# One-engine norm chains, heads with k outermost, and later table steps in a nine-layer block on one core

## The chip, the cores and the metric

The kernel runs on one core of a Trainium2 chip. The metric is the device time of one execution in microseconds. A core has the engines PE (matrix multiplication), DVE (VectorE), ACT (ScalarE) and POOL (GpSimd), and SP, which here only issues DMA transfers.

## The reference

Two blocks of two layers work on x, 512 tokens of 1024 channels, in float32. Every layer is a mixer or a feed-forward part with a residual sum and a normalisation over the channels; cut to what matters:

```
rms_norm(x, g) = x * rsqrt(mean(x*x, -1) + eps) * g
# first block: pool mixer, ffn, attention, ffn, each of them:
m = mixer_or_ffn(rms_norm(x, pre_g))
x = x + rms_norm(m, post_g)
# ffn: u = h @ w_in; width-3 causal conv + bias; gelu(gate) * val; @ w_out
# second block, modulated by a condition c: s5 mixer, mlp, ssd mixer, mlp
h = rms_norm(x, g) * (1 + scale) + shift
x = x + gate * y(h)
# last: rms_norm(x, final_g)
```

The s5 mixer needs powers and phasors of a complex matrix, which depend on the weights alone ("tables").

## The kernel before, in words

The channels lie on the partitions: x is eight tiles (k = 0 to 7) of 128 channels by 512 tokens. Each product is made of three matmuls of rounded halves, `hi*hi`, `lo*hi`, `hi*lo` (L219, L220, L221); the weights' halves `wh`, `wl` are made by ACT (L204) and DVE (L205). The layers are pool, ffn0, attn, ffn1, s5, mlp0, ssd, mlp1 and a final norm.

Between two layers stands a seam (`seam`), in halves of 256 tokens: the tail of the layer before for a half, then for the first block `chain` (`post_add`): a sum of squares of the tail's output `f` (`Norm.add`), its root by two tiny matmuls against ones and a diagonal (`Norm.rs`: L306, ACT's root L309, DVE's reciprocal L310 and diagonal `dg` L313, L319, and ACT's copy to `rs`, L321), then per k tile a scaling of `f` (L449, L450) and the sum into x (L453), and the squares of the new x. For an ffn or attention behind it (`PreScale`) `h` is x times a gain, split into `hi` (ACT, L427) and `lo` (DVE, L428), and the root is applied to the outputs (`un` or `u` times `rsx`, L979 and L952). For the second block (`PreNorm`) `h` needs the root first: L397, L400, `hi` L401, `lo` L402. Alternate k tiles go to POOL and DVE (`engs`); the sums of squares have one accumulator on each (L296). Then the head: the first four (ssd: five) output tiles of the next layer, by halves (`Held.run`), 192 matmuls of 128x256. Two output tiles q = 0, 1 share a PSUM bank; the code takes all k of q = 0, then of q = 1, bank after bank.

The code's order isn't the order on the engines. A scheduler that simulates the engines puts every instruction in a fixed place in its engine's queue; the chains have a raised priority. An engine works through its queue in order, so an instruction that waits holds what is behind it.

The tables of s5 are generators whose steps (up to a `yield`) are taken by the layers: in the pool layer once (`work(1)`), in ffn0 `rate` steps behind each group and one behind each tile of a down projection. A group is two gate and two value tiles: 96 matmuls of 128x512 into four banks, and four `u` (L952). ffn0 has eleven groups (the first is the head's) in three phases, with a down projection after each.

Of the kernel before, what the change touches and what calls it, by code (L numbers as in the profile page):

```python
# [63 lines left out]
def net_kernel(ctx: ExitStack, tc: tile.TileContext, I: dict, out: bass.AP, parts=ALL):  # L64
# [165 lines left out]

    def project(W, k0, nk, c0, tiles, xh, xl, evac, **kw):

        for n in range(tiles[0], tiles[1], 2):
# [44 lines left out]
    class Norm:  # L278
        def __init__(self):
            self.acc = {}  # L280
            self.seen = set()

        def add(self, tile_, span, eng):
            a, b = span
            if eng not in self.acc:
                self.acc[eng] = tt("acc")
            dst = self.acc[eng][:, a:b]
            if (eng, a) not in self.seen:
                self.seen.add((eng, a))
                if span == FULL:  # L290
                    self.seen.add((eng, HALVES[1][0]))
# [6 lines left out]
        def rs(self, span, eps, out=None):  # L298
# [15 lines left out]
            if nb == 2:  # L314
                p2 = ps[:, 256:]
            else:
                p2 = psn.tile([P, 512], F32, tag="n", name=nm("pn"))
# [53 lines left out]
    class PreNorm:  # L371
# [15 lines left out]
        def run(self, span):  # L387
# [25 lines left out]
    class PreScale(PreNorm):  # L413
# [16 lines left out]
        def run(self, span):  # L430
            if self.rs is None:
                self.rs = xp.tile([P, S], F32, tag="rsx", name=nm("rsx"))
            self.norm.rs(span, self.eps, out=self.rs)

    def engs(k):
        return G if k % 2 else V

    def post_add(ft, sq, gname, g0, span, nxt, pre):

        ts = slice(*span)  # L440
        for k in POOL_K:
            A.activation(ft[k][:, ts], ft[k][:, ts], AF.Copy, scale=vc(gname, g0 + k))
# [113 lines left out]
    def s5_powers(pool, dr, pr, pi, cr, ci, sg, far, near):  # L556
# [1496 lines left out]
```

## Time and profile before

| | us |
|---|---|
| median of three runs | 2519.96 (2519.84 to 2521.32) |
| the profiled execution | 2522.2 |
| its span, first to last instruction | 2520.5 |
| PE busy | 2358.8 (94%) |
| DVE busy | 1717.7 (68%) |
| ACT busy | 1151.8 (46%) |
| POOL busy | 454.9 (18%) |

The time outside the span is 1.7 us. The mean granted clock of TensorE is 0.968 of full. PE's busy time contains matmuls at the lower of its two clocks and matmuls whose ends are modelled, so it is read together with the granted clock and the start times of neighbours. An engine's idle time is named with what released it: `<-DVE u L952 14.2` means 14.2 us of waiting that ended with DVE's operation of line 952.

### The profile page before, as it was taken

To read this page: it belongs to the slowest core of one execution; us is meant where nothing else is said; L and a number is where in the kernel's file an instruction comes from. 1 tells how busy PE (TensorE), PEld (TensorE's weight loads), DVE (VectorE), ACT (ScalarE), POOL (GpSimd) and SP (SyncE) were. 2 spreads that over 40 slices of the span, in tenths; PEclk is the share of its full clock that TensorE was granted. 3 is DMA by queue.
4 is the path that set the end of the run, shared out by engine and by line. 5 is a ranking of instruction groups with operands and counts; after the bars stand their busy time and mean duration, and the time that the engine had idled before them with its cause. 6 is when DMAs were issued, how large, how long until landed. Compare 5 with 4: busy or idle time off the path is not lost.

```text
span 2520.5 us, 33869 instructions
## 1 busy us (share of the span) xinstructions
PE 2358.8 (94%) x12485; PEld 1986.4 (79%) x12485; DVE 1717.7 (68%) x2969; ACT 1151.8 (46%) x2070; POOL 454.9 (18%) x489
## 2 busy tenths in 40 slices
PE   6889999988889999996899999999999999999998
PEld 5767777876677888886878887788877888888888
DVE  6895987677858778777654666666778788633333
ACT  6443534467676444354543432333555554422322
POOL 2202131131321000014111210112133432301110
PEclk9989999989999999997999999999999999999999
DMA  4234443312094555551952356543333332233322
GB/s 123 67 100 131 125 138 112 122 43 67 27 231 136 176 175 167 184 176 56 304 158 76 114 167 195 178 149 97 110 101 97 111 103 82 91 100 97 96 88 72
DMA packets 297782, 311.32 MB, mean 124 GB/s; under 512 B 53569, under 2 KB 251025, under 8 KB 296593
## 3 DMA queue, kind: packets, MB, share of 16 engines
q1 hardware_dynamic: 270033, 278.22, 35.5%
q10 hardware_dynamic: 23680, 17.31, 2.3%
q0 software_dynamic: 3904, 13.63, 1.6%
q8 instruction: 98, 1.61, 0.3%
q14 instruction: 67, 0.55, 0.1%
HBM read 284.92 MB, written 24.18 MB: 123 GB/s over the span
## 4 chain that ended last, share of the span: by engine, by line
PE 70%; DVE 12%; DMA 7%; ACT 5%; issue 4%; POOL 1%; SPq 0%; DVEq 0%; ACTq 0%; POOLq 0%
PE mm L220 20%; PE mm L219 20%; PE mm L221 20%; DMA as<-in_ada_w 4%; DVE wl L205 2%; DVE aa L504 1%; DMA tz<-d_k 1%; ACT wh L204 1%; PE pb L1725 1%; PE mm L1655 1%; DVE u L450 1%; PE mm L1656 1%; PE mm L1657 1%; PE pn L306 1%; PE pb L765 1%
## 5 line engine op out<-in xcount | busy, mean ns | idle before, releaser
L219 PE MATMUL mm<-h,wh 128*128 128x512 f32 (+1 forms) x1792 | 665.0, 374 | 40.5 <-DVE u L952 14.2
L220 PE MATMUL mm<-h,wh 128*128 128x512 f32 (+1 forms) x1792 | 668.3, 374 | 24.8 <-DVE h L428 12.6
L221 PE MATMUL mm<-h,wl 128*128 128x512 f32 (+1 forms) x1792 | 665.7, 372 | 1.9 <-DVE wl L205 1.9
L204 ACT ACTIVATE wh<-ws 128x1024 fp32r<-128x1024 f32 (+1 forms) x367 | 387.6, 1059 | 563.7 <-PE mm L220 490.4
L205 DVE TENSOR_TENSOR wl<-ws,wh 128x1024 fp32r<-128x1024 f32 (+1 forms) x367 | 467.2, 1277 | 256.0 <-ACT wh L204 247.6
L219 PEld LDWEIGHTS mm<-h,wh 128*128 128x128 f32 x1792 | 348.0, 195 | 97.6 <-issue 16.9
L220 PEld LDWEIGHTS mm<-h,wh 128*128 128x128 f32 x1792 | 348.3, 195 | 83.6 <-DVE h L428 15.5
L221 PEld LDWEIGHTS mm<-h,wl 128*128 128x128 f32 x1792 | 348.9, 195 | 57.0 <-DVE wl L205 2.5
L219 PE MATMUL mm<-hi,wh 128*128 128x512 f32 (+1 forms) x1056 | 370.9, 356 | 10.1 <-ACT wh L204 9.6
L220 PE MATMUL mm<-lo,wh 128*128 128x512 f32 (+1 forms) x1056 | 371.9, 354 | 1.6 <-DVE lo L328 1.5
L221 PE MATMUL mm<-hi,wl 128*128 128x512 f32 (+1 forms) x1056 | 371.0, 353 | 0.2 <-DVE wl L205 0.2
L219 PEld LDWEIGHTS mm<-hi,wh 128*128 128x128 f32 x1056 | 201.3, 191 | 37.8 <-ACT wh L204 10.9
L220 PEld LDWEIGHTS mm<-lo,wh 128*128 128x128 f32 x1056 | 202.2, 191 | 28.4 <-DVE lo L328 2.6
L221 PEld LDWEIGHTS mm<-hi,wl 128*128 128x128 f32 x1056 | 201.4, 191 | 26.8 <-DVE wl L205 0.7
L504 DVE SCALAR_TENSOR_TENSOR aa<-as,cond,aa 128x512 f32<-128x512 f32 x168 | 130.5, 777 | 113.3 <-DMA as<-in_ada_w 112.1
L1279 POOL TENSOR_TENSOR r<-r 128x512 f32<-128x512 f32 x64 | 85.7, 1343 | 520.1 <-ACT r L1275 445.3
L771 POOL TENSOR_TENSOR dd<-ident,s5dg 16x64 f32<-16x64 f32 x16 | 56.6, 3539 | 327.5 <-DVE kt L773 320.3
L296 POOL TENSOR_TENSOR acc<-acc,sq 128x256 f32<-128x256 f32 (+1 forms) x64 | 58.5, 916 | 302.8 <-ACT sq L295 292.4
L328 DVE TENSOR_TENSOR lo<-r,hi 128x512 fp32r<-128x512 f32 x64 | 47.2, 743 | 76.9 <-ACT hi L326 76.9
L1300 DVE SCALAR_TENSOR_TENSOR x<-mm,mod,x 128x512 f32<-128x512 f32 (+1 forms) x76 | 48.9, 662 | 62.5 <-PE mm L221 62.4
L512 ACT ACTIVATE ab<-aa 128x512 bf16<-128x512 f32 x72 | 45.0, 625 | 89.5 <-DVE aa L504 49.8
L326 ACT ACTIVATE hi<-r 128x512 fp32r<-128x512 f32 x64 | 40.1, 630 | 70.1 <-POOL r L1279 70.1
(491 smaller groups left out, 3822.7 us busy)
## 6 DMA issues: line engine op xcount, KB each, us to landing
ws<-in_mlp_w SPq DMA_DIRECT2D x124, 512.0 KB, 4.0
as<-in_ada_w SPq DMA_DIRECT2D x192, 256.0 KB, 3.1
ws<-in_ffn_w_in SPq DMA_DIRECT2D x88, 512.0 KB, 4.4
ws<-in_m_w_in SPq DMA_DIRECT2D x41, 512.0 KB, 3.7
ws<-in_ffn_w_out SPq DMA_DIRECT2D x40, 512.0 KB, 3.8
ws<-in_w_o SPq DMA_DIRECT2D x16, 512.0 KB, 3.7
ct<-d_tab SPq DMA_DIRECT2D x8, 1024.0 KB, 6.2
ws<-in_s_w_glu SPq DMA_DIRECT2D x16, 512.0 KB, 6.3
```

The costliest lines, as they stand in the source:

```text
L204: A.activation(h_, s_, AF.Copy)
L205: V.tensor_tensor(l_, s_, f(h_), ALU.subtract)
L219: T.matmul(ps, wh, xh, start=first, stop=False)
L220: T.matmul(ps, wh, xl, start=False, stop=False)
L221: return T.matmul(ps, wl, xh, start=False, stop=last).ins
L296: eng.tensor_tensor(dst, dst, sq[:, a:b], ALU.add)
L328: return hi_, V.tensor_tensor(lo[:, ts], src, f(hi[:, ts]), ALU.subtract)
L504: V.scalar_tensor_tensor(acc, st, col(k), acc, ALU.mult, ALU.add)
L512: A.activation(parts[j], acc, AF.Copy)
L771: G.tensor_tensor(dd, ident[:16, :16].unsqueeze(1).broadcast_to([16, 4, 16]), dg[:, g4].unsqueeze(2).broadcast_to([16, 4, 16]), ALU.mult)
L1279: G.tensor_tensor(r, r, r, ALU.mult)
L1300: V.scalar_tensor_tensor(xT[n][:, ts], ps, md(i, 5, n), xT[n][:, ts], ALU.mult, ALU.add)
```

## The change

Line numbers move by a few: after the change the weight matmuls are L218 to L220, the ones-matmuls L329 and L338, the scaling and the sum of `post_add` L460 and L463, `lo` of `PreScale` L445, the two DVE operations of `PreNorm` L414 and L418, the sums of squares L321, `u` L965 and `un` L992.

Three things change.

1. The chains. All elementwise steps are on DVE instead of alternating with POOL; one accumulator of squares instead of two, so half as many ones-matmuls. DVE reads the root from PSUM; ACT's copy to `rs` is left only for `PreScale`'s output factor. `PreNorm` has per k tile one DVE operation (x times gain times root), ACT's `hi` with the shift as its bias, and one DVE operation for `lo`; four operations before. ACT's scaling of two `f` tiles for POOL goes. The lags between the stages are new.
2. The heads. `run_abreast` takes k outermost over all output tiles of the head in two banks (ssd: three), 12 matmuls a k tile. Keys and values of the attention do the same.
3. The tables. Their code has more `yield`s; the step of the pool layer goes, ffn0 begins with 2 steps instead of `rate`, and `rate` is 5 instead of 4.

```diff
-POST_LAGS = (0, 2, 3, 4)
-PRE_LAGS = (0, 1, 1, 3)
-POOL_K = (2, 5)
+POST_LAGS = (0, 1, 2, 3)
+PRE_LAGS = (0, 1, 2)
...
+    def mm_abreast(banks, xh, xl, nk, span):
+
+
+        ts = slice(*span)
+        for k in range(nk):
+            for ps, chs, nq in banks:
+                wh, wl, k0, _ = next(ch for ch in chs if ch[2] <= k < ch[2] + ch[3])
+                for q in range(nq):
+                    qs = slice(q * P, (q + 1) * P)
+                    ins = mm3(ps[:, 256 * q:256 * q + 256], wh[:, k - k0, qs], wl[:, k - k0, qs], xh[k][:, ts],
+                              xl[k][:, ts], k == 0 and q == 0, k == nk - 1 and q == nq - 1)
+        return ins
...
+        def run_abreast(self, hf, xh, xl, evac):
...
+            nq = [kw.get("ncol", 256) // P for *_, kw in self.runs]
+            ps = [psmm() for _ in self.runs]
+            mm_abreast([(p, self.ch[i], n) for i, (p, n) in enumerate(zip(ps, nq))], xh, xl, self.runs[0][2],
+                       HALVES[hf])
...
-                eng.tensor_tensor(dst, dst, sq[:, a:b], ALU.add)
+                V.tensor_tensor(dst, dst, sq[:, a:b], ALU.add)
...
-            out = tt("rs") if out is None else out
-            A.activation(out[:, a:b], p2[:, :b - a], AF.Copy)
             return out
...
-                return engs(k).tensor_tensor(us[k], xT[k][:, ts], rs[:, ts], ALU.mult)
+                return V.scalar_tensor_tensor(us[k], xT[k][:, ts], self.gs[:, k:k + 1], rs, ALU.mult, ALU.mult)
...
-                    lambda k: V.tensor_scalar(us[k], us[k], self.gs[:, k:k + 1], md(i, m, k), ALU.mult, ALU.add),
-                    lambda k: A.activation(self.h[k][0][:, ts], us[k], AF.Copy),
-                    lambda k: V.tensor_tensor(self.h[k][1][:, ts], us[k], f(self.h[k][0][:, ts]), ALU.subtract)),
+                    lambda k: A.activation(self.h[k][0][:, ts], us[k], AF.Identity, bias=md(i, m, k)),
+                    lambda k: V.scalar_tensor_tensor(self.h[k][1][:, ts], us[k], md(i, m, k), f(self.h[k][0][:, ts]),
+                                                     ALU.add, ALU.subtract)),
...
-            if k in POOL_K:
-                return G.tensor_tensor(us[k], ft[k][:, ts], rs[:, ts], ALU.mult)
-            return V.scalar_tensor_tensor(us[k], ft[k][:, ts], vc(gname, g0 + k), rs[:, ts], ALU.mult, ALU.mult)
+            return V.scalar_tensor_tensor(us[k], ft[k][:, ts], vc(gname, g0 + k), rs, ALU.mult, ALU.mult)
...
-                with behind(last):
-                    work(1)
...
-            hd.run(hf, pre.hi, pre.lo, evac)
+            hd.run_abreast(hf, pre.hi, pre.lo, evac)
...
-            bg[0](rate)
+            bg[0](2)
...
-                              lambda: rope_c.update(rope_tables()) if "attn" in names else None, 4)
+                              lambda: rope_c.update(rope_tables()) if "attn" in names else None, 5)
```

How the order on the engines moves, at three places. First PE at the seam from ffn0 to attn, in the head of half 0 (`h_44..` are the `h` tiles, `mm_..` the output tiles, `pn` the root of half 1). Before:

```order
L221 MATMUL mm_5054<-h_4406,wl_5041 128x256
L219 MATMUL mm_5054<-h_4408,wh_5040 128x256
L319 MATMUL pn_4873<-dg_4881,ones 128x128 x2
L220 MATMUL mm_5054<-h_4409,wh_5040 128x256
L221 MATMUL mm_5054<-h_4408,wl_5041 128x256
L219 MATMUL mm_5054<-h_4410,wh_5040 128x256
```

After:

```order
L218 MATMUL mm_5034<-h_4400,wh_5020 128x256
L219 MATMUL mm_5034<-h_4401,wh_5020 128x256
L220 MATMUL mm_5034<-h_4400,wl_5021 128x256
L329 MATMUL pn_4859<-ones,acc_4448 128x128 x2
L338 MATMUL pn_4859<-dg_4865,ones 128x128 x2
L218 MATMUL mm_5153<-h_4386,wh_4984 128x256
L218 MATMUL mm_5154<-h_4386,wh_5008 128x256
```

The matmuls of the root of half 1 stood among the head's, the ones-matmuls 29 rows ahead of the diagonal's; now both stand behind the head's last one, and in front of the head of half 1.

Second, DVE at the seam from pool to ffn0, at the chain of half 0 (`scr`, `er`, `nr`, `ni` are table work, `vec` transposed vectors, `dl` the pool layer's own). Before:

```order
L475 SCALAR_TENSOR_TENSOR scr_507<-scr_507,er_498 128x64
L146 COPY vec<-mm_818 128x128
L146 COPY vec<-mm_821 128x128
L146 COPY vec<-mm_824 128x128
L313 TENSOR_SCALAR dg_669<-ident,sr_666 128x128 x2
L478 SCALAR_TENSOR_TENSOR er_498<-scr_507 128x64
L205 TENSOR_TENSOR wl_959<-ws_957,wh_958 128x1024
L146 COPY vec<-mm_827 128x128
L595 TENSOR_TENSOR nr_529<-er_498,cm_524 128x64
L596 TENSOR_TENSOR ni_530<-er_498,sn_523 128x64
L146 COPY vec<-mm_830 128x80
L450 SCALAR_TENSOR_TENSOR u_676<-f_370,vec,rs_674 128x256
```

After:

```order
L332 RECIPROCAL sr_564<-sr_564 128x2
L335 TENSOR_SCALAR dg_567<-ident,sr_564 128x128 x2
L917 SCALAR_TENSOR_TENSOR dl_322<-mm_502,vec,dh_321 128x256
L917 SCALAR_TENSOR_TENSOR dl_333<-mm_512,vec,dh_332 128x256
L923 COPY x_100<-mm_512 128x256
L917 SCALAR_TENSOR_TENSOR dl_344<-mm_522,vec,dh_343 128x256
L460 SCALAR_TENSOR_TENSOR u_572<-f_370,vec,pn_561 128x256
L460 SCALAR_TENSOR_TENSOR u_574<-f_380,vec,pn_561 128x256
```

Before, 49 rows, most of them table work, stand between the reciprocal and `dg`; now none.

Third, DVE in ffn0 in front of the first `u` (`s5ph`, `cm`, `ea`, `th`, `er`, `sc` are table work). Before:

```order
L621 TENSOR_TENSOR s5ph_459<-s5ph_459,t_117_538 128x64x4
L618 TENSOR_TENSOR s5ph_458<-s5ph_458,ea_495 128x64x4
L623 TENSOR_TENSOR s5ph_459<-s5ph_459,cm_1311 128x64x2
L619 TENSOR_TENSOR cm_1323<-s5ph_459,t_117_538 128x256
L952 TENSOR_TENSOR u_1454<-mm_1330,rsx_910 128x512
L952 TENSOR_TENSOR u_1456<-mm_1332,rsx_910 128x512
```

After:

```order
L470 TENSOR_SCALAR sc_1135<-th_1134 128x64
L479 TENSOR_SCALAR scr_1145<-er_1136 128x64
L471 TENSOR_SCALAR sc_1135<-sc_1135 128x64
L480 TENSOR_SCALAR scr_1145<-scr_1145 128x64
L965 TENSOR_TENSOR u_1285<-mm_1161,rsx_805 128x512
L473 SCALAR_TENSOR_TENSOR th_1134<-sc_1135,th_1134 128x64
```

Before, 111 rows stand between the last `un` and the first `u`, the powers up to the phasors among them; now 36, and the table work goes on behind it at an earlier point of its own sequence.

## Rows read from the trace of the kernel before

**Rows 1.** The page, busy time of each engine, share of the span, instructions:

```profile
PE 2358.8 (94%) x12485; PEld 1986.4 (79%) x12485; DVE 1717.7 (68%) x2969; ACT 1151.8 (46%) x2070; POOL 454.9 (18%) x489
```

**Rows 2.** Instructions by line and form: count, busy us, mean ns, idle before and releaser:

```profile
L219 PE MATMUL mm<-h,wh 128*128 128x512 f32 x1360 | 534.9, 394 | 15.4 <-DVE u L952 14.2 <-DVE kr L1093 1.3
L220 PE MATMUL mm<-h,wh 128*128 128x256 f32 x432 | 135.4, 316 | 24.8 <-DVE h L428 12.6 <-DVE h L402 12.1
```

**Rows 3.** Busy time in stretches: length, each engine (count), granted clock, DMA share, GB/s:

```profile
102.00:134.00 32.00, 18.80 (x83) 15.22 (x82) 31.42 (x113) 10.46 (x13) 0.00 (x0) 0.84 0.30 94
...
121.00:142.00 21.00, 7.04 (x19) 5.60 (x20) 20.50 (x78) 4.34 (x6) 0.00 (x0) 0.59 0.14 42
...
142.00:208.00 66.00, 66.00 (x297) 52.50 (x296) 62.85 (x104) 33.82 (x58) 10.43 (x2) 1.00 0.43 127
...
51.00:99.00 48.00, 34.77 (x241) 32.33 (x240) 39.80 (x90) 23.82 (x56) 18.97 (x25) 0.86 0.11 34
...
504.00:551.00 47.00, 35.86 (x240) 33.25 (x240) 33.99 (x73) 22.74 (x64) 21.70 (x24) 0.82 0.08 25
...
1136.00:1194.00 58.00, 37.70 (x230) 35.40 (x231) 41.60 (x77) 22.01 (x50) 25.84 (x35) 0.71 0.14 46
1367.00:1406.00 39.00, 30.37 (x207) 29.11 (x207) 24.21 (x53) 17.18 (x35) 9.56 (x11) 0.82 0.12 36
...
2148.00:2180.00 32.00, 28.42 (x206) 27.39 (x205) 23.47 (x51) 14.19 (x33) 8.64 (x9) 0.89 0.14 41
```

**Rows 4.** Timeline of PE in ffn0: start, duration, what, idle before:

```profile
134.97 0.77 PE L219 MATMUL mm<-h,wh 128*128 128x512 f32 x1 [14.16 <-DVE u L952]
135.53 0.63 PE L220 MATMUL mm<-h,wh 128*128 128x512 f32 x1
135.96 0.63 PE L221 MATMUL mm<-h,wl 128*128 128x512 f32 x1
```

**Rows 5.** Timeline of PE, seam from ffn0 to attn:

```profile
503.21 0.28 PE L220 MATMUL mm<-lo,wh 128*128 128x256 f32 x1
503.33 0.28 PE L221 MATMUL mm<-hi,wl 128*128 128x256 f32 x1
...
505.65 1.19 PE L306 MATMUL pn<-ones,acc 128*128 128x128 f32 x6 [1.33 <-POOL acc L296]
...
511.74 0.79 PE L219 MATMUL mm<-h,wh 128*128 128x256 f32 x2 [2.73 <-ACT h L427]
...
515.35 0.41 PE L219 MATMUL mm<-h,wh 128*128 128x256 f32 x1
515.56 0.41 PE L220 MATMUL mm<-h,wh 128*128 128x256 f32 x1
...
535.82 0.39 PE L220 MATMUL mm<-h,wh 128*128 128x256 f32 x1 [2.51 <-DVE h L428]
```

**Rows 6.** Timelines of ACT and POOL, the same seam:

```profile
509.04 0.38 ACT L321 ACTIVATE rs<-pn 128x256 f32<-128x256 f32 x1 [1.90 <-PE pn L319]
...
516.58 3.20 POOL L453 TENSOR_TENSOR x<-x,u 128x256 f32<-128x256 f32 x1 [2.16 <-DVE u L450]
```

**Rows 7.** Timeline of DVE, seam from pool to ffn0:

```profile
41.51 0.15 DVE L310 RECIPROCAL sr<-sr 128x2 f32<-128x2 f32 x1
...
53.09 0.47 DVE L313 TENSOR_SCALAR dg<-ident,sr 128x128 f32<-128x128 f32 x2
```

**Rows 8.** Timeline of PE, seam from ffn1 to s5:

```profile
1141.49 2.08 PE L306 MATMUL pn<-ones,acc 128*128 128x128 f32 x8 [5.74 <-DVE acc L296]
...
1170.89 2.23 PE L306 MATMUL pn<-ones,acc 128*128 128x128 f32 x8 [5.21 <-DVE acc L296]
```

**Rows 9.** Timeline of DVE, sums in the attention's chain, and `un` from PSUM:

```profile
510.83 0.41 DVE L453 TENSOR_TENSOR x<-x,u 128x256 f32<-128x256 f32 x1
...
512.90 0.94 DVE L453 TENSOR_TENSOR x<-x,u 128x256 f32<-128x256 f32 x1
...
95.84 1.41 DVE L979 TENSOR_TENSOR un<-mm,rsx 128x256 f32<-128x256 f32 x4
```

More of the change, by code (lines that the diff above doesn't have):

```diff
@@ L263, in load_run @@
             self.ch[i] += self.ap[i]
+        def run_abreast(self, hf, xh, xl, evac):
+            for i in range(len(self.runs)):
+                if i not in self.ch:
+                    self.load_run(i)
+            nq = [kw.get("ncol", 256) // P for *_, kw in self.runs]
+            ps = [psmm() for _ in self.runs]
+            mm_abreast([(p, self.ch[i], n) for i, (p, n) in enumerate(zip(ps, nq))], xh, xl, self.runs[0][2],
+                       HALVES[hf])
+            for i, n in enumerate(nq):
+                for q in range(n):
+                    evac(i, q, ps[i][:, 256 * q:256 * q + 256], HALVES[hf])
         def run(self, hf, xh, xl, evac):
@@ L295, in add, with rs @@
                 A.activation(sq[:, a:b], tile_[:, a:b], AF.Square)
-                eng.tensor_tensor(dst, dst, sq[:, a:b], ALU.add)
-        def rs(self, span, eps, out=None):
+                V.tensor_tensor(dst, dst, sq[:, a:b], ALU.add)
+        def rs(self, span, eps):
             a, b = span
             nb = (b - a) // P
-            accs = list(self.acc.values())
             ps = psn.tile([P, 512], F32, tag="n", name=nm("pn"))
             for j in range(nb):
-                for i, acc in enumerate(accs):
-                    T.matmul(ps[:, j * P:(j + 1) * P], acc[:, a + j * P:a + (j + 1) * P], ones,
-                             start=i == 0, stop=i == len(accs) - 1)
+                T.matmul(ps[:, j * P:(j + 1) * P], self.acc[:, a + j * P:a + (j + 1) * P], ones, start=True, stop=True)
             sr = cst.tile([P, 4], F32, tag="nsr", bufs=2, name=nm("sr"))
@@ L313, in rs @@
                 V.tensor_scalar(dg[:, j * P:(j + 1) * P], ident, sr[:, j:j + 1], None, ALU.mult)
[L314 to L317, printed above, removed]
+            out = ps[:, 256:256 + (b - a)]
             for j in range(nb):
-                T.matmul(p2[:, j * P:(j + 1) * P], ones, dg[:, j * P:(j + 1) * P], start=True, stop=True)
-            out = tt("rs") if out is None else out
-            A.activation(out[:, a:b], p2[:, :b - a], AF.Copy)
+                T.matmul(out[:, j * P:(j + 1) * P], ones, dg[:, j * P:(j + 1) * P], start=True, stop=True)
             return out
@@ L432, in run @@
                 self.rs = xp.tile([P, S], F32, tag="rsx", name=nm("rsx"))
-            self.norm.rs(span, self.eps, out=self.rs)
-    def engs(k):
-        return G if k % 2 else V
+            A.activation(self.rs[:, slice(*span)], self.norm.rs(span, self.eps), AF.Copy)
     def post_add(ft, sq, gname, g0, span, nxt, pre):
         ts = slice(*span)
-        for k in POOL_K:
-            A.activation(ft[k][:, ts], ft[k][:, ts], AF.Copy, scale=vc(gname, g0 + k))
         rs = sq.rs(span, eps1)
@@ L914, in tail_ @@
             if hf == 0:
-                last = banded(0)
+                banded(0)
             a, b = HALVES[hf]
@@ L1294, in evac @@
                     squared(rs.pop((i, q)))
-            hd.run(hf, pre.hi, pre.lo, evac)
+            hd.run_abreast(hf, pre.hi, pre.lo, evac)
         def down(n, ps, span, nxt=None):
@@ L1301, in down @@
             if nxt is not None:
-                nxt.add(xT[n], span, engs(n))
+                nxt.add(xT[n], span)
             bg[0](1)
@@ L1420, in head @@
             S_["pre"] = pre
-            hd.run(hf, pre.hi, pre.lo, lambda i, q, ps, span: u_out(2 * i + q, ps, span))
+            hd.run_abreast(hf, pre.hi, pre.lo, lambda i, q, ps, span: u_out(2 * i + q, ps, span))
         def glu_mm(pp, chs, ks):
@@ L1441, in glu @@
             if S_["nxt"] is not None:
-                S_["nxt"].add(xT[n], span, engs(n))
+                S_["nxt"].add(xT[n], span)
         def body_():
@@ L1681, in o_evac @@
             if S_["nxt"] is not None:
-                S_["nxt"].add(xT[n], span, engs(n))
+                S_["nxt"].add(xT[n], span)
         def bcast(a, o, d=64):
@@ L1806, in evac @@
                 A.activation(raw[i][:, slice(*span)], ps, AF.Copy)
[L1808 removed]
+            hd.run_abreast(hf, pre.hi, pre.lo, evac)
             if hf:
@@ L1908, in chain @@
             for k in range(KD):
-                nxt.add(xT[k], span, engs(k))
+                nxt.add(xT[k], span)
     work = Background()
```

39 lines of the change are left out of this document (20 added, 19 removed).

## The prediction

> **What bounds the kernel now.** The first page lines [rows 1] say that PE is busy for 94% of the span, so the time can fall only where PE stands still or runs at the slower of its two clocks. I then read the list of instructions by line, for the idle time in front of the weight matmuls [rows 2]: one wait of 14.2 us for the DVE operation `u` of L952, and, for the 256-token matmuls of the heads, 24.8 us of waits for `h` from DVE on L220 alone. Then the busy time by stretches [rows 3], with a stretch for each seam, from the last matmul of a tail to the last matmul of the head after it: they take 48, 47, 58, 39 and 32 us, and the granted clock in them is 0.71 to 0.89 of full. A head has 192 matmuls of 128x256; two neighbours at the full 2.4 GHz start 0.12 us apart (503.21 and 503.33), at 1.2 GHz 0.21 us apart (515.35 and 515.56) [rows 5]. So a head wants 23 us, and each seam above pays 9 to 35 us for waits and for the slower clock. I name them by the layers: pool-ffn0 (51 to 99), ffn0-attn (504 to 551), ffn1-s5 (1136 to 1194), s5-mlp0 (1367 to 1406), ssd-mlp1 (2148 to 2180). The seams attn-ffn1 and mlp0-ssd have the same pattern and lose less.
>
> All sums are against the profiled execution: span 2520.5 us, 2522.2 us in all, which is 2.2 us above the median of 2519.96; a saving is taken off the median unchanged.
>
> **The table steps, ffn0.** Between the last `un` of the head and the first `u`, DVE is busy for 31.42 of 32 us [rows 3], while PE runs out of work at 120.8 and waits 14.16 us; after it the clock is at 1.2 GHz, matmuls of 512 columns starting 0.43 us apart [rows 4], where 297 in 66 us (0.22 us each) is the usual pace [rows 3]. The granted clock is 0.59 from 121 to 142 [rows 3], that is 1.2 GHz for 17 of the 21 us, of which some 6 lie behind the wait and lose 3 more: 17 us in all. In the new order 36 DVE rows instead of 111 stand between the last `un` and the first `u`. With the traced durations of their kinds they sum to 13 us, less than the 22 us of PE work there (96 matmuls at 0.22), so this wait goes. What is late next: the same table work is spread over the groups of the first phase, and the stretch 142 to 208 has DVE busy 62.85 of 66 us already [rows 3]. Summed in the same way from the head's end, the first `u` of the next three groups stands on DVE at 15, 43 and 70 us; PE needs its bank back at 22, 44 and 65. The third is 5 us late, and the clock after such a wait may cost 2 more: I leave 7 and take **10 us gained** (bounds 4 and 17).
>
> **pool-ffn0.** Here table operations stand inside the chain. The reciprocal of half 0 runs at 41.51, the diagonal `dg` that needs only it at 53.09 [rows 7], 11.6 us later; then come 2.6 us to the first `u`. The new order has `dg` right behind the reciprocal, five rows ahead of the first L460. The chain of half 0, three DVE operations a k tile plus the sum, 31 at a start-to-start 0.34 to 0.40 us, thus runs under the pool's last matmuls, and head(0) can begin at about 53 instead of 58 and run at PE's pace: 12 matmuls a k tile are 1.44 us, three DVE operations 1.1. I put its end at 65. Then half 1's sum and `rs` (5 us, below), and 11.5 us and 1.5 of slow clock: 83 against 99, **16 us gained** (bounds 8 and 20).
>
> **ffn0-attn.** The bare chain, from the end of the ones-matmuls (505.65 + 1.19) to the first `h` matmul at 511.74, is 4.9 us [rows 5]; it loses ACT's copy of `rs` (0.38 us [rows 6]), since DVE now reads PSUM. Head(0) had its `h` late because POOL held one `x` for 3.20 us [rows 6], and a DVE operation beside a POOL one takes 0.94 instead of 0.41 [rows 9]. All on DVE, a k tile costs 1.1 us, less than its 12 matmuls, so PE sets the pace: 40 matmuls at 0.21 up to 520, 56 at 0.12, end at 526.5. Now the loss. Before, the second output tile of each bank (48 matmuls) stood behind the first and the ones-matmuls of half 1 among them; now both stand behind the last matmul of head(0), so PE waits for the bare chain: 4.5 us and 0.5 for the matmuls themselves, to 531.5. Then 96 matmuls, 11.5 us, and 1.5 for a slow stretch like the one around the present wait of 2.51 us [rows 5]: 544.5 against 551, **6.5 us gained** (bounds 0 and 10).
>
> **The other seams.** ffn1-s5 has two chains in series, with waits of 5.74 and 5.21 us for the sum alone [rows 8]. POOL's part goes, but DVE then runs 16 operations, 7 sums, 16 more, and by the new order the second ones-matmuls of half 0 and half 1 stand behind the last tail matmul and behind head(0), where before 72 tail matmuls followed them: first `h` at +14 instead of +13 us, head(0) to +29, second chain 14 us, head(1) 15 with half of it slow: 58. **0** (bounds -6 and +8). s5-mlp0: one normalisation with two DVE operations (0.8 us a k tile) instead of four over two engines; head(0) ends at about 1383, `rs` 5, head(1) 13: **5 us gained** (1 to 8). ssd-mlp1: 2148 + 1 + 12 + 5 + 11.5 = 2177.5, **3 us** (-1 to 6). attn-ffn1 and mlp0-ssd: **2 and 1** by the same pattern (each -2 to 4).
>
> A price that I set to nothing: DVE reading `rs` from PSUM. Four operations with a PSUM operand take 1.41 us together, 0.35 a piece [rows 9], as SBUF ones do. [...] Extra sums on DVE (62 of 0.34 us) lie in the tails, beside matmuls, except the last of each half, which the chains above count.
>
> **Sum.** 10 + 16 + 6.5 + 0 + 5 + 3 + 2 + 1 = 43.5, about 43: 2522.2 becomes 2479, the median **2477 us** (-1.7%).
>
> **Rivals.** (A) The forecast, chance 0.57, its own range 2463 to 2490. (B) Exposed `rs` waits send the clock down at each half. Speaks for it: the waits of 5 us in ffn1-s5 [rows 8] go with a clock of 0.71 there [rows 3]. Half of a head at 0.21 instead of 0.12 is 48 x 0.09 = 4.3 us, 3 more than A has, in six seams, and the tables give 6 less: -43 + 24 = -19, 2501. Chance 0.17. (C) Production stops limiting anything: the clock stays full, the third group's `u` is on time: 7 more from the tables, 3 from each of five seams: -65, 2455. Chance 0.12. (D) Slower: the heads were PE-bound already. Before, the banks alternate by k in the static order too, so if k outermost gives them nothing, each of the seven seams pays the uncovered `rs`, 5 us and up to 4 of slow clock, against some 4 that it waits today (2.51 for DVE's `h` [rows 5] and less for ACT's): 7 x 5 = +35. With the tables and the pool chain at their lower bounds (4 and 8) it is about +23, 2543; it decides the sign once a seam loses over 1.7 us on average. Against it: head(0) of ffn0-attn takes 19 us where its matmuls want 11.5. Chance 0.08. (E) The scheduler gives the same heads and the table wait only moves to the third group: gains and losses cancel, 2520. Chance 0.06.
>
> **How the numbers follow.** The prediction is A. The range 2455 to 2503 takes A, the upper half of C and the lower part of B. A difference under 0.2% (5 us) can't be told from none here. A, B and C are faster, with a little of B lost to the rest: 0.85; same 0.06; slower 0.09.
>
> **What would show it.** PE's wait of 14 us for `u` is gone, and a wait under 7 us for the third group's first `u` stands in its place. POOL has no 128x256 operation in a seam; DVE's take 0.41 to 0.48 throughout. Head(0) of ffn0-attn runs in 15 us or less, then PE waits 4.5 to 5 us for `rs`. pool-ffn0 ends by 84. If heads still run at over 0.16 us a matmul with DVE idle, it is the clock (B); if DVE is busy without a break there, production was mis-sized. A seam that is longer than before in three places would make D right.

## The result, and the profile after

The changed kernel takes 2489.89 us (median, 2489.15 to 2495.89) against 2520.64 for the kernel before on the same chip: a ratio of 0.988, interval 0.9861 to 0.9899, 31 us less where 43 were forecast. A second measurement on another chip, where the kernel before takes 2528.77, gave 2494.16 (2493.28 to 2499.14), ratio 0.9867 (0.985 to 0.9883). The time lies in the stated range; but the parts of the sum came out otherwise than forecast, and most of what follows is about them. The profiled execution after is one of 2495.9 us, span 2494.2, so its sum against the 2520.5 of before is 26.3.

The page, as [rows 1]: PE's share is the same, and POOL has lost a quarter of its work.

```profile
PE 2340.0 (94%) x12397; PEld 1970.8 (79%) x12397; DVE 1712.5 (69%) x3069; ACT 1139.7 (46%) x2038; POOL 340.0 (14%) x345
```

The seven stretches from the last matmul of a tail to the last matmul of the head, in the columns of [rows 3]:

```profile
49.00:82.00 33.00, 28.45 (x217) 27.36 (x217) 27.29 (x72) 18.50 (x47) 0.00 (x0) 0.95 0.18 54
485.00:529.00 44.00, 33.41 (x220) 31.77 (x220) 34.49 (x100) 20.42 (x59) 0.00 (x0) 0.81 0.12 36
707.00:755.00 48.00, 33.74 (x245) 31.71 (x245) 29.88 (x71) 28.69 (x53) 0.00 (x0) 0.86 0.68 164
1121.00:1181.00 60.00, 34.53 (x221) 32.74 (x220) 41.17 (x99) 23.87 (x50) 3.26 (x9) 0.72 0.21 71
1355.00:1388.00 33.00, 28.12 (x202) 27.20 (x201) 20.03 (x45) 16.36 (x31) 0.00 (x0) 0.90 0.18 56
1726.00:1750.00 24.00, 21.86 (x153) 21.07 (x153) 12.71 (x30) 7.91 (x18) 0.00 (x0) 0.86 0.23 66
2125.00:2154.00 29.00, 26.92 (x206) 26.20 (x205) 19.28 (x45) 13.39 (x30) 0.00 (x0) 0.94 0.23 69
```

The lengths stand in the first column of numbers; against [rows 3] the first seam falls from 48 to 33 us, the clock in it rises from 0.86 to 0.95, and POOL is empty in nearly all. Read to a tenth from the timelines of the two profiled executions, where a body is what lies between two seams:

| us | before | after | change | forecast |
|---|---|---|---|---|
| pool, to the end of its tail | 51.3 | 49.6 | -1.7 | |
| pool-ffn0 | 47.7 | 32.8 | -14.9 | -16 |
| ffn0 body (with the table wait) | 404.6 | 402.7 | -1.9 | -10 |
| ffn0-attn | 47.4 | 43.6 | -3.8 | -6.5 |
| attn body | 184.9 | 178.3 | -6.6 | 0 |
| attn-ffn1 | 42.9 | 48.1 | +5.2 | -2 |
| ffn1 body | 356.9 | 365.7 | +8.8 | 0 |
| ffn1-s5 | 58.0 | 59.8 | +1.8 | 0 |
| s5 body | 173.2 | 174.6 | +1.4 | 0 |
| s5-mlp0 | 38.7 | 33.1 | -5.6 | -5 |
| mlp0 body | 340.1 | 337.5 | -2.6 | 0 |
| mlp0-ssd | 28.2 | 24.3 | -3.9 | -1 |
| ssd body | 373.8 | 375.1 | +1.3 | 0 |
| ssd-mlp1 | 32.2 | 28.6 | -3.6 | -3 |
| mlp1 and final | 340.5 | 340.5 | 0 | 0 |

Where the terms come from is seen line by line. DVE in pool-ffn0, which answers to [rows 7] (start, duration, what):

```profile
39.95 0.15 DVE L332 RECIPROCAL sr<-sr 128x2 f32<-128x2 f32 x1
40.14 0.48 DVE L335 TENSOR_SCALAR dg<-ident,sr 128x128 f32<-128x128 f32 x2
...
43.53 0.87 DVE L460 SCALAR_TENSOR_TENSOR u<-f,vec,pn 128x256 f32<-128x256 f32 x2 [0.23 <-PE pn L338]
```

The diagonal follows its reciprocal by 0.2 us instead of 11.6, the first `u` by 3.6, and the chain runs under the tail.

PE in ffn0, the place of [rows 4]; and DVE's operation that it waits for:

```profile
160.72 0.76 PE L218 MATMUL mm<-hi,wh 128*128 128x512 f32 x1 [6.43 <-DVE u L965]
...
159.89 1.28 DVE L965 TENSOR_TENSOR u<-mm,rsx 128x512 f32<-128x512 f32 x2
```

The wait of 14.16 us is gone; 6.43 us stand at the third group's first `u`, as forecast. At the layer's end PE waits longer for the weights' halves than before, 7.0 us against 4.3 in the last 60 us; the longest of these waits, after the change:

```profile
442.13 0.58 PE L218 MATMUL mm<-hi,wh 128*128 128x256 f32 x1 [2.06 <-ACT wh L203]
```

And the head's end has something new (PE, the roots of half 1 for `rsx`, in pool-ffn0 and in attn-ffn1):

```profile
82.18 0.61 PE L329 MATMUL pn<-ones,acc 128*128 128x128 f32 x4
...
85.53 1.17 PE L338 MATMUL pn<-dg,ones 128*128 128x128 f32 x4 [2.75 <-DVE dg L335]
...
754.81 0.61 PE L329 MATMUL pn<-ones,acc 128*128 128x128 f32 x4
...
758.17 1.19 PE L338 MATMUL pn<-dg,ones 128*128 128x128 f32 x4 [2.74 <-DVE dg L335]
```

Nothing stands between the two in PE's queue any more, and PE waits for ACT and DVE in between. In ffn0-attn, which answers to [rows 5]:

```profile
488.43 1.23 PE L329 MATMUL pn<-ones,acc 128*128 128x128 f32 x4 [3.43 <-DVE acc L321]
490.62 1.19 PE L338 MATMUL pn<-dg,ones 128*128 128x128 f32 x4 [0.97 <-DVE dg L335]
493.56 0.80 PE L218 MATMUL mm<-h,wh 128*128 128x256 f32 x2 [1.75 <-ACT h L444]
...
507.88 0.61 PE L329 MATMUL pn<-ones,acc 128*128 128x128 f32 x4
509.46 0.68 PE L338 MATMUL pn<-dg,ones 128*128 128x128 f32 x4 [0.97 <-DVE dg L335]
511.89 0.53 PE L218 MATMUL mm<-h,wh 128*128 128x256 f32 x2 [1.75 <-ACT h L444]
```

The first sum is late now (3.43 us where PE waited 1.33 before; all sums are on DVE's queue). Head(0) runs from 493.56 to 508.04, 14.5 us for its 96 matmuls instead of 18.9, and then 3.8 us pass for the bare root, where 5 were worked out. And attn-ffn1, where the largest miss among the seams is (ACT and PE):

```profile
727.62 0.33 ACTq L802 DMA_DIRECT2D d_tab<-th  x1
734.14 2.03 ACT L801 ACTIVATE th<-tz 128x1024 f32<-128x1024 f32 x1 [6.34 <-DMA d_tab<-th]
735.97 0.22 ACT L331 ACTIVATE sr<-pn,eps 128x2 f32<-128x2 f32 x1
...
736.86 1.20 PE L338 MATMUL pn<-dg,ones 128*128 128x128 f32 x4 [7.77 <-DVE dg L335]
```

The label on PE's wait names `dg`, but its cause is two engines back: the last copy `th` of another table has one buffer and waits for the transfer that empties it, and the root `sr` of half 1 stands behind it on ACT. In the order before, this `sr` stood two rows ahead of that `th`; in the new order it stands right behind it. Before (ACT and PE):

```profile
754.30 0.26 ACT L309 ACTIVATE sr<-pn,eps 128x2 f32<-128x2 f32 x1 [0.40 <-ACT th L786]
...
759.32 2.06 ACT L786 ACTIVATE th<-tz 128x1024 f32<-128x1024 f32 x1 [2.92 <-DMA d_tab<-th]
...
762.49 0.80 PE L219 MATMUL mm<-h,wh 128*128 128x256 f32 x2 [4.88 <-ACT h L427]
```

So the copy held up PE before as well, but only at ACT's first `h`, when the root was done: 4.88 us. From the end of head(0) to the start of head(1) it took 7.2 us then and takes 12.2 now, which is the seam's loss.

### The profile page after: what moved, and what is told of

It reads as the page before. It is cut to its first block, busy times and chain, and to the rows that moved or that the text cites. A ratio compares the mean times of both kernels' runs of the same rounds, so it can differ in the third digit from the quotient of the medians.

```text
span 2494.2 us, 33556 instructions
## 1 busy us (share of the span) xinstructions
PE 2340.0 (94%) x12397; PEld 1970.8 (79%) x12397; DVE 1712.5 (69%) x3069; ACT 1139.7 (46%) x2038; POOL 340.0 (14%) x345
## 4 chain that ended last, share of the span: by engine, by line
PE 71%; DVE 13%; DMA 8%; ACT 4%; issue 4%; SPq 0%; POOL 0%; DVEq 0%; ACTq 0%; POOLq 0%
PE mm L219 21%; PE mm L218 21%; PE mm L220 20%; DMA as<-in_ada_w 5%; DVE wl L204 3%; ACT wh L203 1%; DVE aa L514 1%; DMA tz<-d_k 1%; PE mm L1665 1%; PE mm L1666 1%; PE mm L1667 1%; PE pb L1735 1%; PE pb L780 1%; DMA d_tab<-th 1%; PE pn L338 1%
## 5 line engine op out<-in xcount | busy, mean ns | idle before, releaser
L218 PE MATMUL mm<-h,wh 128*128 128x512 f32 (+1 forms) x1792 | 661.5, 373 | 18.3 <-ACT h L444 7.2
L220 PE MATMUL mm<-h,wl 128*128 128x512 f32 (+1 forms) x1792 | 664.4, 372 | 1.0 <-DVE wl L204 1.0
L218 PEld LDWEIGHTS mm<-h,wh 128*128 128x128 f32 x1792 | 345.4, 195 | 75.6 <-ACT h L417 8.4
L220 PEld LDWEIGHTS mm<-h,wl 128*128 128x128 f32 x1792 | 347.9, 194 | 55.8 <-DVE wl L204 1.6
L218 PE MATMUL mm<-hi,wh 128*128 128x512 f32 (+1 forms) x1056 | 370.8, 355 | 14.6 <-ACT wh L203 6.8
L220 PE MATMUL mm<-hi,wl 128*128 128x512 f32 (+1 forms) x1056 | 372.2, 354 | 1.5 <-DVE wl L204 1.5
L218 PEld LDWEIGHTS mm<-hi,wh 128*128 128x128 f32 x1056 | 201.5, 191 | 43.2 <-ACT wh L203 8.2
L219 PEld LDWEIGHTS mm<-lo,wh 128*128 128x128 f32 x1056 | 202.3, 192 | 28.6 <-DVE lo L345 2.6
L220 PEld LDWEIGHTS mm<-hi,wl 128*128 128x128 f32 x1056 | 202.2, 192 | 28.2 <-DVE wl L204 2.0
L786 POOL TENSOR_TENSOR dd<-ident,s5dg 16x64 f32<-16x64 f32 x16 | 69.4, 4338 | 344.2 <-DVE kt L788 336.9
L321 DVE TENSOR_TENSOR acc<-acc,sq 128x256 f32<-128x256 f32 (+1 forms) x148 | 63.9, 443 | 17.3 <-ACT sq L320 13.0
```

The source lines that it names most:

```text
L218: T.matmul(ps, wh, xh, start=first, stop=False)
L219: T.matmul(ps, wh, xl, start=False, stop=False)
L220: return T.matmul(ps, wl, xh, start=False, stop=last).ins
L321: V.tensor_tensor(dst, dst, sq[:, a:b], ALU.add)
L786: G.tensor_tensor(dd, ident[:16, :16].unsqueeze(1).broadcast_to([16, 4, 16]), dg[:, g4].unsqueeze(2).broadcast_to([16, 4, 16]), ALU.mult)
```

## The experiments

The kernels of one group ran beside the kernel before on one chip; that took 2528.8, 2528.0 and 2525.3 us there, so times are compared as differences from it.

| run | median us | from before | ratio (interval) |
|---|---|---|---|
| again (the change) | 2494.2 | -34.6 | 0.9867 (0.985 to 0.9883) |
| heads_undone | 2488.4 | -40.4 | 0.9839 (0.9825 to 0.9854) |
| tables_undone | 2506.1 | -22.7 | 0.9905 (0.989 to 0.992) |
| chains_undone | 2529.6 | +0.9 | 1.0005 (0.9995 to 1.0014) |
| chains_alone | 2496.5 | -31.5 | 0.9878 (0.9857 to 0.9899) |
| tables_alone | 2521.8 | -6.2 | 0.9976 (0.9967 to 0.9986) |
| root_copied | 2499.5 | -28.6 | 0.9881 (0.9856 to 0.9906) |
| adds_on_pool | 2498.7 | -29.3 | 0.9888 (0.987 to 0.9906) |
| only_keys_abreast | 2484.3 | -41.0 | 0.9839 (0.9823 to 0.9854) |
| root_later | 2488.4 | -36.9 | 0.985 (0.9833 to 0.9867) |
| two_sums | 2488.0 | -37.4 | 0.9849 (0.9831 to 0.9866) |
| four_step_norm | 2524.3 | -1.1 | 0.9999 (0.9988 to 1.0011) |

### Spread: again

No edit.

> The changed kernel itself, once more, for its spread: three of its four runs took 2489.2 to 2490.1 us and the profiled one 2495.9. In that one ACT stood for 6.34 us behind a write to d_tab in the seam from attn to ffn1, with the root of half 1 behind it. If that was one slow transfer, the wait is short here and the profiled run takes about 2490; if it belongs to the order of the queues, it stands here again and the run takes about 2496.

The wait on ACT stands here too, in the same place:

```profile
729.47 2.03 ACT L801 ACTIVATE th<-tz 128x1024 f32<-128x1024 f32 x1 [5.96 <-DMA d_tab<-th]
731.30 0.22 ACT L331 ACTIVATE sr<-pn,eps 128x2 f32<-128x2 f32 x1
```

So it belongs to the order of ACT's queue, not to one slow transfer. PE's wait for this root is 4.7 to 8.0 us in five further kernels with the new chains as well (heads_undone, tables_undone, chains_alone, only_keys_abreast, root_later), and in all of them ACT has `sr` right behind that `th`, which waits 3.9 to 6.7 us for the write. In adds_on_pool (below) `sr` (738.26) happens to stand ahead of that `th` (743.65): there is no wait in front of this L338, and the seam takes 42.9 us instead of the 46.6 of again.

### Which part carries the gain: heads, tables, chains

heads_undone:

```diff
-            hd.run_abreast(hf, pre.hi, pre.lo, evac)
+            hd.run(hf, pre.hi, pre.lo, evac)
```

(in all heads, and keys and values bank after bank again.)

> The changed kernel with the heads (and keys and values) tile after tile as before; chains and tables stay as changed. My theory: k outermost lets PE run at the pace of the chain and is worth about 2 us in each of seven seams, so some 2504 us. The rival (the second tile of each bank had covered the root of half 1, and the uncovered wait costs 5 us a seam): 2470 to 2480. If the scheduler's order makes no difference to a head: 2490.

Against my theory, which had it 14 us slower than the changed kernel (2504 against 2490): it is faster by 5.7 us on the same chip, the four runs of the one (2485.6 to 2491.6) below the four of the other. So k outermost costs something, but less than the rival had, and not where the rival had it. The heads of the two are alike: head(0) of ffn0-attn takes 15.0 us tile after tile and 14.5 with k outermost, and the bare root of half 1 stands in front of head(1) in both. What differs is the end of the head:

```profile
756.74 0.61 PE L329 MATMUL pn<-ones,acc 128*128 128x128 f32 x4
...
759.08 0.68 PE L338 MATMUL pn<-dg,ones 128*128 128x128 f32 x4 [0.90 <-DVE dg L335]
```

Here the wait of 2.74 us in attn-ffn1 is 0.90 (and 0.90 for 2.74 in pool-ffn0), and the body of ffn1 is 6.4 us shorter than in again. The attention's body is 6.9 us longer.

tables_undone: rate 4, `work(1)` in the pool layer, fewer yields; of its edits:

```diff
-            bg[0](2)
+            bg[0](rate)
```

> The changed kernel with the table steps as before (rate 4, the step in the pool layer, fewer yields); chains and heads stay as changed. My theory: the wait for the first u in ffn0 comes back (7 us net by the trace of the changed kernel) and so does the table work in the chain from pool to ffn0 (about 10 us): 2507 us. The rival, that the moved table work costs in ffn0 what it gives in front of it: 2490.

12 us slower than the changed kernel, where the theory had 17 (7 and 10, from 2490 to 2507; on this chip the changed kernel takes 2494.2). pool-ffn0 is 42.3 us instead of 32.8, and the wait is back at its old place, one group behind the head:

```profile
131.85 0.76 PE L218 MATMUL mm<-h,wh 128*128 128x512 f32 x1 [10.74 <-DVE u L962]
```

chains_undone: the kernel before with `run_abreast` and the new table steps, so that against the changed kernel the chains alone are old:

```diff
-            return V.scalar_tensor_tensor(us[k], ft[k][:, ts], vc(gname, g0 + k), rs, ALU.mult, ALU.mult)
+            if k in POOL_K:
+                return G.tensor_tensor(us[k], ft[k][:, ts], rs[:, ts], ALU.mult)
...
-                return V.scalar_tensor_tensor(us[k], xT[k][:, ts], self.gs[:, k:k + 1], rs, ALU.mult, ALU.mult)
+                return engs(k).tensor_tensor(us[k], xT[k][:, ts], rs[:, ts], ALU.mult)
```

> The changed kernel with the chains as before (POOL and DVE, two accumulators, the root copied to SBUF, four operations in PreNorm); heads and tables stay as changed. My theory: the chains on DVE alone give about 2 to 3 us a seam, 15 to 20 in all: 2505 to 2510 us. The rival, that heads and tables give all of it: 2490.

All of the gain is gone, 35 us and not 15 to 20: the seams are 38.7, 46.8, 40.9, 64.5, 38.3, 27.6 and 34.5 us, together 23 us more than in again, and the bodies take 11 more. Behind the old chains the heads with k outermost gain little: head(0) of ffn0-attn takes 18.1 us (18.9 before, 19.2 in tables_alone), that of pool-ffn0 14.1 (16.1 in tables_alone).

chains_alone: the new chains in the kernel before; of the edits against the changed kernel:

```diff
-            hd.run_abreast(hf, pre.hi, pre.lo, evac)
+            hd.run(hf, pre.hi, pre.lo, evac)
...
-            bg[0](2)
+            bg[0](rate)
```

> The kernel before with the new chains alone: heads tile after tile, table steps as before. The undoings so far give, against the kernel before on the same chip: all three parts -34 us, without the heads -40, without the tables -23, without the chains 0. If the parts add up, the chains alone give 35 less what the pair of tables and heads needs of them: -29 (-40 from chains and tables, +11 for the tables). The rival, that the tables' gain comes only when the chains have freed DVE and so part of the 35 is the tables': -20 or less.

tables_alone: the new table steps in the kernel before; of the edits against that:

```diff
-                with behind(last):
-                    work(1)
...
-            bg[0](rate)
+            bg[0](2)
```

> The kernel before with the new table steps alone. In the chains_undone run (tables and heads new) the seam from pool to ffn0 ended 9.7 us earlier than before, and the whole was level. My theory: the tables give about 6 us (1.3 to 12) there and the heads took it back: -6. The rival, that without the lighter chains the table work costs DVE as much in ffn0 as it gives in front: 0.

Both as my theory had it (-31.5 and -6.2). With them the seven kernels agree on a nearly additive account: the chains give 32 to 36 us, the tables 6 to 12 (more, the lighter the chain), and k outermost takes 6 to 9 whatever the rest (tables and heads, 0.9 against -6.2 of the tables alone; chains and heads, -22.7 against -31.5; all three, -34.6 against -40.4). The heads alone were not run.

Where k outermost takes it can be read from the profiled executions of these three pairs. The seven seams together are between 1.1 us longer and 4.4 us shorter with it, the bodies 4.9 to 16.0 us longer. One piece lies in s5, whose head's outputs are written out and read back as `U` (PE, again):

```profile
1188.98 1.97 PE L1383 MATMUL pv<-U,vt 128*128 128x128 f32 x16 [1.05 <-DMA U<-d_u]
```

In all nine kernels here with k outermost in the heads, PE waits 0.9 to 2.1 us for this transfer and 14.2 to 16.2 us in the whole body of s5; in the five with the heads tile after tile it is 0 to 0.5 and 10.9 to 12.9.

### What in the chains: PSUM, POOL, the sums, the number of steps

root_copied:

```diff
+            r_ = tt("rs")
+            A.activation(r_[:, a:b], out, AF.Copy)
+            return r_[:, a:b]
-            return out
```

> The changed kernel with ACT's copy of the root to SBUF put back, which DVE then reads; all else as changed. My theory: a DVE operation costs the same from PSUM (L460, L414: 473 and 474 ns) as from SBUF, and the copy costs each chain 0.4 to 0.8 us on the path: 12 chains, +5 to +9 us, the two DVE groups still at 470 to 475 ns. [...]

The DVE groups that read the root, from PSUM in again and from SBUF here (instructions by line, mean ns behind the comma):

```profile
L460 DVE SCALAR_TENSOR_TENSOR u<-f,vec,pn 128x256 f32<-128x256 f32 x64 | 29.7, 475 | 7.7 <-PE pn L338 7.7
L414 DVE SCALAR_TENSOR_TENSOR u<-x,gs,pn 128x256 f32<-128x256 f32 x64 | 29.1, 475 | 6.7 <-PE pn L338 6.7
```

```profile
L464 DVE SCALAR_TENSOR_TENSOR u<-f,vec,rs 128x256 f32<-128x256 f32 x64 | 30.0, 479 | 15.5 <-ACT rs L341 15.5
L418 DVE SCALAR_TENSOR_TENSOR u<-x,gs,rs 128x256 f32<-128x256 f32 x64 | 29.4, 480 | 10.4 <-ACT rs L341 10.4
```

475 ns from PSUM against 479 and 480 from SBUF: for this operation, with one operand in PSUM, the root read there costs nothing more. DVE waits 11.5 us longer in front of the two groups (15.5 + 10.4 against 7.7 + 6.7). The time is some 6 us longer, with intervals that overlap; that is in line with the theory and proves no size.

adds_on_pool:

```diff
-    staged((norm, lambda k: V.tensor_tensor(xT[k][:, ts], xT[k][:, ts], us[k], ALU.add)) + parts,
+    staged((norm, lambda k: (G if k % 2 else V).tensor_tensor(xT[k][:, ts], xT[k][:, ts], us[k], ALU.add)) + parts,
```

> The changed kernel with every second sum into x (32 of 64) on POOL again, all else as changed: DVE has 13 us less to do. My theory: POOL's operations make those of DVE beside them twice as long (0.94 for 0.41 us before), and POOL's own take 0.85 us and more in the chain: L460 and L445 rise to a mean of 0.55 us or more and the time by 8 to 15 us. The rival, that the gain was the shorter chain (fewer steps, fewer hand-offs) and not POOL's absence: level, within 3 us, or faster.

```profile
L463 POOL TENSOR_TENSOR x<-x,u 128x256 f32<-128x256 f32 x32 | 30.4, 949 | 182.7 <-DVE u L460 182.7
...
L460 DVE SCALAR_TENSOR_TENSOR u<-f,vec,pn 128x256 f32<-128x256 f32 x64 | 28.6, 472 | 9.6 <-PE pn L338 9.6
...
L445 DVE SCALAR_TENSOR_TENSOR h<-x,vec,h 128x256 fp32r<-128x256 f32 x32 | 17.3, 549 | 3.5 <-ACT h L444 3.5
...
L463 DVE TENSOR_TENSOR x<-x,u 128x256 f32<-128x256 f32 x32 | 16.0, 500 | 0.0
```

Here POOL does stretch what runs on DVE beside it (L445 from 476 in the profiled execution after to 549, the sums from 418 to 500 ns), L460, with one operand in PSUM, not at all (475 and 472), and POOL's sums take 949 ns; but the four seams with these sums come to 177.6 us, less than the 182.3 of again; 3.7 of that is attn-ffn1, where ACT's order fell better. The whole is 5 us longer, with intervals that overlap, neither the theory's 8 to 15 nor level; in the profiled executions the bodies alone are longer, by 12 us. So my theory that POOL's sums into x held the seams falls. That DVE's 32 operations fewer make up for the longer ones is likely, but not shown.

two_sums: the sums of squares on two engines again, all else as changed.

```diff
-                V.tensor_tensor(dst, dst, sq[:, a:b], ALU.add)
+                eng.tensor_tensor(dst, dst, sq[:, a:b], ALU.add)
```

> The changed kernel with the sums of squares again in two accumulators, one on DVE and one on POOL (62 POOL operations, twice the ones-matmuls); all else as changed. If the single sum on DVE is where the chains gain, the seams ffn1-s5, s5-mlp0, mlp0-ssd and ssd-mlp1 grow by 2 us each and the whole by 8 to 15 us. The rival: DVE has the room on either side and POOL's sums are hidden in the tails: within 3 us.

```profile
L322 POOL TENSOR_TENSOR acc<-acc,sq 128x256 f32<-128x256 f32 x62 | 53.8, 870 | 410.2 <-ACT sq L321 388.1 <-issue 16.0 <-DMA ws<-in_m_w_in 4.8
L322 DVE TENSOR_TENSOR acc<-acc,sq 128x256 f32<-128x256 f32 x62 | 34.0, 554 | 10.6 <-ACT sq L321 9.3
```

Against the theory: the four seams that it named are 1.2 to 2.2 us shorter than in again, ffn0-attn is 2.9 shorter (PE's wait for the first sum there 1.11 us for 3.44), only pool-ffn0 grew clearly, by 2.8; the time is level with the changed kernel or a little below (-37.4 against -34.6, overlapping intervals). The single sum on DVE is not where the chains gain; in five of the seven seams it rather costs.

four_step_norm: `PreNorm` as before, with the copied root; everything else as changed.

```diff
-                return V.scalar_tensor_tensor(us[k], xT[k][:, ts], self.gs[:, k:k + 1], rs, ALU.mult, ALU.mult)
+                return (G if k % 2 else V).tensor_tensor(us[k], xT[k][:, ts], rs[:, ts], ALU.mult)
```

> The changed kernel with PreNorm as before (root copied to SBUF, x times root on POOL and DVE in turn, a second DVE operation, ACT, a third DVE operation); post_add and the sums stay as changed. My theory: the three seams whose only chain this is (s5-mlp0, mlp0-ssd, ssd-mlp1) lose what they won, 5.6, 4.4 and 3.3 us, ffn1-s5 as much, 13 to 20 us in all; the other seams stay. The rival, that the gain there came from the single sum and k outermost: within 3 us.

The whole gain is gone, 33 us and not 13 to 20. Against again the four seams with this norm are 4.2, 3.7, 3.7 and 7.4 us longer (63.6, 36.8, 27.5 and 36.3), 19 us, which is the theory's; the bodies of s5 and ssd between them are 9.2 us longer, and what comes before, where the code is the same, 3.5. In ssd-mlp1, PE's timeline here, then that of again:

```profile
2153.14 0.58 PE L219 MATMUL mm<-h,wh 128*128 128x256 f32 x1 [4.07 <-DVE h L421]
...
2169.82 0.50 PE L218 MATMUL mm<-h,wh 128*128 128x256 f32 x2 [2.17 <-ACT h L420]
2172.04 0.58 PE L219 MATMUL mm<-h,wh 128*128 128x256 f32 x1 [1.72 <-DVE h L421]
```

```profile
2136.82 0.68 PE L338 MATMUL pn<-dg,ones 128*128 128x128 f32 x4 [0.97 <-DVE dg L335]
2138.62 0.50 PE L218 MATMUL mm<-h,wh 128*128 128x256 f32 x2 [1.11 <-ACT h L417]
```

The waits for the first `lo` of each half (4.07 and 1.72 us) are there with four steps and not with three. On DVE the first steps run beside POOL's (s5-mlp0; POOL's four `u` take 1362.37 to 1365.99):

```profile
1362.86 0.95 DVE L416 TENSOR_TENSOR u<-x,rs 128x256 f32<-128x256 f32 x1
1363.85 0.69 DVE L419 TENSOR_SCALAR u<-u,gs,mod 128x256 f32<-128x256 f32 x1
```

So the longer way to the first pair of halves is what the second block's seams pay: one more step, ACT's copy of the root, and the first steps at up to double length beside POOL (L416 0.95 us at 1362.86, 0.41 at 1367.86, behind POOL's last). Which of these weighs most was not told apart. Taken by whole times, nearly all of the chains' 35 us hang on this norm, though the first block's chains are still new here and pool-ffn0 and ffn0-attn as short as in again. The 9 us of the two bodies are not explained: before, with the old heads, the body of ssd took 373.8 us with the same four steps, and here, with k outermost, 382.5 (382.9 in chains_undone).

### What k outermost costs: two more versions

only_keys_abreast: all heads tile after tile, keys and values with k outermost.

```diff
-            hd.run_abreast(hf, pre.hi, pre.lo, evac)
+            hd.run(hf, pre.hi, pre.lo, evac)
```

> The changed kernel with the seven heads tile after tile, but keys and values still with k outermost. The heads undone altogether gave 2488.4 where the changed kernel took 2494.2 and the kernel before 2528.8 on that chip; in that run the attention's body was 7 us longer than in the changed kernel, all other bodies together 13 us shorter. If the keys and values make that difference, 2482 (46 us under the kernel before); if it only came of the order that the scheduler happened on, 2488 (40 under).

2484.3 us, 41.0 under the kernel before, the largest difference of all, but not the 46 of keys and values, and not told from heads_undone (0.9839 in both). The attention's body is 178.4 us, as in the changed kernel, where it was 182.7 in heads_undone; but chains_alone has 176.9 with keys and values bank after bank, so they are not shown to make the difference.

root_later:

```diff
         after.head(0, pre)
+        if pre.late:
+            pre.run(HALVES[1])
         after.head(1, pre)
```

(and no longer with raised priority.)

> The changed kernel, heads with k outermost, with one thing moved: the root of half 1 for the output factor rsx of PreScale is given out between the two heads and without raised priority, so that some 33 matmuls stand between its two parts in PE's queue in pool-ffn0, ffn0-attn and attn-ffn1 where 0 to 4 stood. My theory: the wait in front of L338 at the end of the head (2.75, 1.87 and 2.74 us, with a slower clock behind two of them) is what k outermost costs: the waits go and the time falls by 7 to 10 us against the changed kernel (41 to 44 under the kernel before). The rival, that the cost lies in the heads themselves: level with the changed kernel (34 under).

```profile
754.65 0.61 PE L329 MATMUL pn<-ones,acc 128*128 128x128 f32 x4
...
762.64 0.61 PE L338 MATMUL pn<-dg,ones 128*128 128x128 f32 x4
...
110.52 0.70 PE L218 MATMUL mm<-h,wh 128*128 128x512 f32 x1 [3.58 <-DVE u L966]
...
139.08 0.77 PE L218 MATMUL mm<-h,wh 128*128 128x512 f32 x1 [4.93 <-DVE u L966]
```

In attn-ffn1 the two matmuls of the root are 8 us apart with work between them, no wait is left at the head's end, the granted clock in the 24.3 us behind it is 1.00 (0.93 in again), and the body of ffn1 falls from 366.9 to 358.8 us. In pool-ffn0 the 2.75 us go as well, but PE then waits 3.58 and 4.93 us for `u` instead of once 6.43: L338 now comes at 90.74 (85.33 in again), DVE's last four `un`, which need this root, at 91.80 (86.98), and the table steps and `u` behind them. A wait taken from PE comes back there. In all -36.9 against -34.6: between theory and rival, and the intervals overlap. That the uncovered root is part of the price is shown by ffn1; that it is all of it is not.

## Why the prediction was right, and where it was not

The time lay in the range, on its slow side, 13 us above the point. That it is this near owes something to luck: by the table, the terms that came out slower than forecast add up to 32 us and those that came out faster to 15, and nothing in the prediction made them cancel. By its steps:

- **Table steps.** The mechanism is as said, to the group: the 14.16 us go and 6.43 stand at the third group's `u` (5 were worked out, 7 left for it). The term was mis-sized, 10 forecast and 2 measured in ffn0's body, because the list of what is late next was short. It had no wait for the root of `rsx` at the head's end (2.75 us) and none for the weights' halves at the layer's end (2.7 us more than before); and the clock gave nothing back, since it is low behind the new waits too (0.72 of full from 85 to 91 and 0.68 from 160.7 to 166, after the change; before, behind the old wait, 0.50 from 135 to 140), 0.94 from 82.3 to 110; PE is busy for 386.2 us of the body in both. The 1.2 GHz of this term is an estimate: 512 columns started 0.43 us apart [rows 4] are 1.2 columns a ns, where the granted clock is 0.50; the 2.4 GHz is its double, and no view shows a frequency. At a granted clock of 1.00 the traces have 512 columns 0.23 us apart (142.88 to 159.88, before), and the sums go by such distances alone. tables_undone puts the tables at 12 us in all, but 9.5 of them are in pool-ffn0.
- **pool-ffn0.** 16 forecast, 14.9 in the seam and 1.7 ahead of it. `dg` stands right behind its reciprocal, and the chain runs under the tail. Right; by tables_undone 9.5 us of it are the table work, and the rest comes with the chains and heads (42.3 us with the old tables, 47.7 before).
- **ffn0-attn.** 6.5 forecast, 3.8 measured. Head(0) was sized right (14.5 against 15.2), the bare root too (3.8 against 5). Missing was the first sum, 3.43 us late, since the sums of the tail all go through DVE: the prediction says that the chains count the last sum of each half, but this term goes from the ones-matmuls of before and has no later sum in it. Head(0) began 8.6 us behind the tail, not 7.8; with two sums (two_sums) the seam takes 40.7 us. The larger miss is head(1), 16.7 us, not 13, at a granted clock of 0.80.
- **The reason for it.** I gave the heads' pace to two things at once, DVE alone and 12 matmuls a k tile. chains_undone and heads_undone part them: with the new chains head(0) of ffn0-attn takes 14.2 to 16.0 us in either order, with the old ones 18 to 19; and in the chains, adds_on_pool and two_sums speak against "all on DVE" as the reason of the gain. The weighing of k outermost at a gain was wrong in sign (6 to 9 us cost), and rival D had the place nearly right: it is a root without cover, but that of `rsx` behind the head more than that in front of head(1), and not that alone (s5).
- **attn-ffn1.** -2 forecast, +5.2 measured. I read only PE's and DVE's orders at the seams; on ACT the change put the last `th` copy, which waits for a write, in front of the root. The term had no wait of ACT in it; adds_on_pool, with the two the other way round, has 42.9 us, as before.
- **The second block.** s5-mlp0, ssd-mlp1 (5 and 3 forecast, 5.6 and 3.6 measured) and ffn1-s5 (0, +1.8) were right, mlp0-ssd was better (3.9 for 1). four_step_norm shows that here the new norm is the cause.
- **PSUM at no price.** Right: 475 ns from PSUM (again), 479 and 480 from SBUF (root_copied).
- **Not in the sum:** the attention's body (-6.6), whose cause stays open, and ffn1's (+8.8), which is for the most part the uncovered root of `rsx` (358.8 us in root_later, 356.9 before).

## What to carry to other kernels

A chain that a matmul engine waits for is judged by the way to its first tile: here a norm with fewer steps and no copy of the root, off POOL, gave 19 us in four seams, while the sums that were moved from POOL to DVE gave none. Before two loops are put into one order, look at what the end of the one had covered: a pair of small matmuls with steps on two other engines between them wants other matmuls there (bare, PE waited 2.75 us in pool-ffn0; in root_later none of it was left at the head's end). And where a scheduler fixes the order, read every engine's queue at the place, since a copy that waits for a transfer can come to stand in front of the one short operation that all wait for (7.77 us of PE's time in attn-ffn1).

## What the runs showed that I had not expected

A change of a few lines moves bodies that it does not touch by several us: the body of ssd is 373.8 to 382.9 us over these kernels, that of ffn1 356.9 to 367.1, with the same work in them. The whole order is laid anew each time; of ffn1's spread the root of `rsx` is a part, the rest was not traced. Seams are therefore compared one by one here, and differences of under 5 us between two whole kernels are not read as the price of an edit.
